# Reading the streamed operand of two chained transformer blocks' matmuls as two interleaved halves

## The chip, the cores and the metric

One core of a Trainium2 chip runs the whole program. The metric is the time of one execution on the device in microseconds, as a median over runs. Engines are named as the profile names them: PE is TensorE's matmul stream, PEld its weight loads, DVE is VectorE, ACT is ScalarE, POOL is GpSimd, SP is the queue that issues DMAs. A matmul has a stationary operand of 128 x 128 (loaded by PEld) and a moving operand of up to 512 columns that streams past it; the sums land in PSUM.

## What is computed

Two transformer blocks on 256 tokens of width 2048, in float32. The first block mixes tokens in three families of heads, then runs a gated convolutional feed-forward (width 5632) and a gated per-layer embedding. The second has a modulation vector, a mixer with windowed and latent attention, and a feed-forward with a squared ReLU (width 8192). Cut to the products around the change:

```
first:   g = conv(h @ w_gate);  y = gelu(g) * (h @ w_up);  x = x + y @ w_down
second:  mod = silu(c) @ w_mod + b_mod          (six rows: sh1, sc1, g1, sh2, sc2, g2)
         u = relu(h @ w_ff1);   x = x + g2 * ((u * u) @ w_ff2)
```

## The kernel before, in words

Weights stream from HBM once. `prep` (lines 273 to 283) fetches one block of 128 x 1024 float32 into `raw`, and splits it into a high part `whi` (ACT, line 281) and a remainder `wlo` (DVE, line 282), both typed float32r. Activations are kept as such pairs too, and each product is three matmuls: high by high, high by low, low by high. There are four `raw` buffers and three of `whi` and `wlo`.

Two helpers issue nearly all matmuls:

- `linear` (lines 297 to 344) has the tokens stationary and the weights moving: 12 matmuls of 512 columns (of 448 or 384 in two chunks) for a block, lines 318, 319, 320. It serves w_in, w_out, w_down, the embedding's products, the second block's w_in2, w_out2, w_ff2, and chunk 0 of ff1. Output has the tokens on partitions.
- `linear_t` (lines 346 to 365) has the weights stationary and the 256 tokens moving: 24 matmuls of 256 columns for a block, lines 360, 361, 362. It serves w_gate, w_up and chunks 1 to 15 of w_ff1. Output has features on partitions and two groups of 256 tokens side by side in a PSUM bank.

Each chunk of 512 outputs is eight blocks. In `linear_t`'s callers the evictions read that bank as `(j t)`: line 984 (gate, DVE), line 1003 (up, DVE), lines 1424 and 1425 (ff1, ACT then DVE).

After each block `tick` (line 250) counts down deferred work that was handed to `spawn`; a deferred piece says after how many ticks it goes on. `tick` also calls `mod_half` at a rate: one of 192 halves of the modulation, a DMA of 512 KB into one of two `wmod` buffers (line 919) and one DVE instruction of 128 x 1024 (line 920). `mod_upto` issues all halves up to a number at once. `mod_row` (lines 935 to 947) adds up a section of the modulation (lines 931, 932), waits 2 ticks, transposes it on PE (line 940), copies it on ACT and spreads it over the partitions through a DRAM row with two kinds of SP DMA.

In `mlp2` the feed-forward runs in four groups of four chunks: ff1 of chunk 4g, then ff2 of the group before, then ff1 of the other three. The last 32 halves of the modulation run at one a tick from the end of ff1's chunk 0. After ff1 of chunk 4 comes `mod_upto(96)`, the `mod_row` for `g2`, and then ff2, whose evictions multiply by `g2`. `out_proj2` calls `mod_row` for `g1` in the same manner.

## Time and profile before

| what | value |
|---|---|
| median of 3 runs | 2290.66 us (2286.03 to 2298.77) |
| profiled execution, its own time | 2293.44 us |
| its span, first to last instruction | 2291.7 us |
| mean granted TensorE clock | 0.993 |
| PE / PEld / DVE / ACT busy | 2246.7 / 1996.9 / 1573.5 / 1105.6 us |
| HBM traffic | 513.38 MB read, 2.14 MB written |

Busy times are sums over instructions. A matmul's row shows its own start and a modelled end, and rows of successive matmuls overlap: the pace of the PE is read from the distance between two starts, not from the duration of one row.

### The profile page before, as it was taken

The page shows a single profiled execution, that of the slowest core. Times are in us where ns is not written, and L with a number is a line of the kernel's source. Part 1 is how long each engine was busy: PE and PEld are TensorE (multiplying, and loading weights), DVE is VectorE, ACT ScalarE, POOL GpSimd, SP SyncE. Part 2 cuts the span into 40 slices and gives each one's busy share as a digit, 9 for nine tenths or more (in the row PEclk, how much of TensorE's full clock was granted, in tenths as well). Part 3 has the DMA queues.
Part 4 walks back from the last instruction along what each step waited for, and adds up shares of the span by engine and source line. Part 5 has one row for each costly group of instructions (what it writes and reads, how often), then busy time and mean ns, then how long its engine had stood idle before and what let it go on. Part 6 is the DMA issues. An engine that isn't in the chain of part 4 may idle for free.

```text
span 2291.7 us, 34932 instructions
## 1 busy us (share of the span) xinstructions
PE 2246.7 (98%) x13714; PEld 1996.9 (87%) x13714; DVE 1573.5 (69%) x2329; ACT 1105.6 (48%) x1560; POOL 25.8 (1%) x35
## 2 busy tenths in 40 slices
PE   9999999999999999999999999999999999999998
PEld 7787887899998999989987788888878998998986
DVE  6777766777876677767777866768766555555555
ACT  6655554454444444434445655655433443443444
POOL 0000000000000000000000000000000000000000
PEclk9999999999999999999999999999999999999999
DMA  8665566677777777777778643566886566656554
GB/s 300 229 211 193 205 230 208 241 254 259 265 264 261 265 252 254 256 258 264 249 255 301 241 161 117 173 194 212 309 290 193 190 187 193 190 187 193 190 188 154
DMA packets 147537, 517.82 MB, mean 226 GB/s; under 512 B 17115, under 2 KB 21292, under 8 KB 146860
## 3 DMA queue, kind: packets, MB, share of 16 engines
q1 hardware_dynamic: 147228, 515.58, 66.3%
q8 instruction: 107, 1.75, 0.3%
q14 instruction: 58, 0.48, 0.1%
q10 hardware_dynamic: 144, 0.01, 0.0%
HBM read 513.38 MB, written 2.14 MB: 225 GB/s over the span
## 4 chain that ended last, share of the span: by engine, by line
PE 80%; DMA 7%; issue 6%; DVE 5%; ACT 1%; POOL 1%; SPq 0%; DVEq 0%; ACTq 0%; POOLq 0%
PE mm L320 14%; PE mm L319 14%; PE mm L318 14%; PE mm L362 11%; PE mm L361 11%; PE mm L360 11%; DMA wmod<-in_w_mod 6%; DVE wlo L282 2%; PE aux L382 1%; DVE wmod L920 1%; PE aux L750 1%; ACT whi L281 1%; DMA raw<-in_w_ff 0%; PE aux L824 0%; PE aux L1273 0%
## 5 line engine op out<-in xcount | busy, mean ns | idle before, releaser
L281 ACT ACTIVATE whi<-raw 128x1024 fp32r<-128x1024 f32 (+1 forms) x746 | 785.9, 1055 | 999.0 <-PE mm L320 539.9
L282 DVE TENSOR_TENSOR wlo<-raw,whi 128x1024 fp32r<-128x1024 f32 (+1 forms) x746 | 905.5, 1216 | 503.6 <-ACT whi L281 501.9
L362 PE MATMUL mm<-xt,wlo 128*128 128x256 f32 x2368 | 662.6, 280 | 5.8 <-DVE wlo L282 5.8
L361 PE MATMUL mm<-xt,whi 128*128 128x256 f32 x2368 | 661.5, 279 | 0.0
L360 PE MATMUL mm<-xt,whi 128*128 128x256 f32 x2368 | 661.5, 279 | 0.0
L361 PEld LDWEIGHTS mm<-xt,whi 128*128 128x128 f32 x2368 | 451.0, 190 | 0.3
L362 PEld LDWEIGHTS mm<-xt,wlo 128*128 128x128 f32 x2368 | 444.6, 188 | 7.4 <-DVE wlo L282 7.2
L360 PEld LDWEIGHTS mm<-xt,whi 128*128 128x128 f32 x2368 | 444.6, 188 | 0.3
L319 PE MATMUL mm<-wlo,hid 128*128 128x512 f32 x848 | 331.4, 391 | 1.0 <-DVE wlo L282 1.0
L318 PE MATMUL mm<-whi,hid 128*128 128x512 f32 x848 | 331.6, 391 | 0.0
L320 PE MATMUL mm<-whi,hid 128*128 128x512 f32 x848 | 331.2, 391 | 0.0
L920 DVE SCALAR_TENSOR_TENSOR wmod<-wmod,cact 128x1024 f32<-128x1024 f32 x192 | 234.5, 1221 | 109.3 <-DMA wmod<-in_w_mod 108.5
L318 PE MATMUL mm<-whi,xt 128*128 128x512 f32 (+2 forms) x660 | 260.3, 395 | 0.9 <-ACT whi L281 0.9
L319 PE MATMUL mm<-wlo,xt 128*128 128x512 f32 (+2 forms) x660 | 256.9, 389 | 3.5 <-DVE wlo L282 3.5
L320 PE MATMUL mm<-whi,xt 128*128 128x512 f32 (+2 forms) x660 | 256.3, 389 | 0.0
L319 PEld LDWEIGHTS mm<-wlo,hid 128*128 128x128 f32 x848 | 159.9, 189 | 35.1 <-DVE wlo L282 2.3
L318 PEld LDWEIGHTS mm<-whi,hid 128*128 128x128 f32 x848 | 159.9, 189 | 33.0
L320 PEld LDWEIGHTS mm<-whi,hid 128*128 128x128 f32 x848 | 159.8, 188 | 33.1
L319 PEld LDWEIGHTS mm<-wlo,xt 128*128 128x128 f32 x660 | 124.5, 189 | 29.3 <-DVE wlo L282 6.6
L318 PEld LDWEIGHTS mm<-whi,xt 128*128 128x128 f32 x660 | 124.3, 188 | 24.6 <-ACT whi L281 1.6
L320 PEld LDWEIGHTS mm<-whi,xt 128*128 128x128 f32 x660 | 124.4, 188 | 23.7
L318 PE MATMUL mm<-whi,mix 128*128 128x512 f32 x244 | 97.9, 403 | 0.0
(349 smaller groups left out, 1796.6 us busy)
## 6 DMA issues: line engine op xcount, KB each, us to landing
raw<-in_w_ff SPq DMA_DIRECT2D x256, 512.0 KB, 3.7
wmod<-in_w_mod SPq DMA_DIRECT2D x192, 512.0 KB, 5.0
raw<-in_w_in SPq DMA_DIRECT2D x120, 512.0 KB, 4.1
raw<-in_w_gate SPq DMA_DIRECT2D x88, 512.0 KB, 3.8
raw<-in_w_up SPq DMA_DIRECT2D x88, 512.0 KB, 4.2
raw<-in_w_down SPq DMA_DIRECT2D x88, 512.0 KB, 4.0
raw<-in_w_out SPq DMA_DIRECT2D x64, 512.0 KB, 3.8
raw<-in_w_pg SPq DMA_DIRECT2D x32, 512.0 KB, 4.6
```

Source lines behind the costliest of these rows:

```text
L281: nc.scalar.activation(hi[:, :ncol], raw[:, :ncol], AF.Copy)
L282: nc.vector.tensor_tensor(lo[:, :ncol], raw[:, :ncol], hi[:, :ncol].bitcast(F32), op=ALU.subtract)
L318: nc.tensor.matmul(o, xh[:, sl], wh, start=st and j == 0, stop=False)
L319: nc.tensor.matmul(o, xh[:, sl], wl, start=False, stop=False)
L320: nc.tensor.matmul(o, xl[:, sl], wh, start=False, stop=en and j == 1)
L360: nc.tensor.matmul(o, hi[:, ws], xh, start=first, stop=False, skip_group_check=True)
L361: nc.tensor.matmul(o, hi[:, ws], xl, start=False, stop=False, skip_group_check=True)
L362: nc.tensor.matmul(o, lo[:, ws], xh, start=False, stop=(b == last and j == 1), skip_group_check=True)
L382: self.nc.tensor.transpose(pt[:, j * P:(j + 1) * P], src[:, j * P:(j + 1) * P], self.ident)
L750: nc.tensor.transpose(pt[:, jo * P:(jo + 1) * P], L[:, j * P:(j + 1) * P], self.ident)
L920: nc.vector.scalar_tensor_tensor(raw, raw, 1.0, self.cact[:, us], op0=ALU.mult, op1=ALU.mult, accum_out=self.macc[:, j, u:u + 1])
```

## The change

The layout of the weights on the host, the order in which moving operands are read, and the place of one deferred piece are changed; no matmul is added or removed. A new function gives a view of a row of columns that reads its two halves in turn (column 0, column n/2, column 1, column n/2 + 1, and so on). In `linear` the host stores each block's columns as all even ones, then all odd ones, so that reading the halves in turn gives the natural order, and outputs stay as they were. In `linear_t` the moving tokens are read in turn, so outputs come out in that order, and the evictions of gate, up and ff1 undo it by reading PSUM at a stride of two elements. `mod_upto(96)` and `mod_row` for `g2` go ahead of ff1's chunk 4 instead of behind it, with a wait of 5 ticks in place of 2. The wait for `g1` stays 2.

```diff
-def _pack(w, widths, nk=2):
+def _pack(w, widths, nk=2, turn=()):
...
-        b = w[:, c0:c0 + cw].reshape(k // (nk * P), nk, P, cw).transpose(0, 2, 1, 3)
+        b = w[:, c0:c0 + cw]
+        if n not in turn:
+            b = np.concatenate([b[:, 0::2], b[:, 1::2]], axis=1)
+        b = b.reshape(k // (nk * P), nk, P, cw).transpose(0, 2, 1, 3)
...
-    a["w_gate"] = _pack(sq("w_gate"), [CW] * NF)
+    a["w_gate"] = _pack(sq("w_gate"), [CW] * NF, turn=range(NF))
...
-    a["w_ff1"] = _pack(sq("w_ff1_2"), [CW] * NF2)
+    a["w_ff1"] = _pack(sq("w_ff1_2"), [CW] * NF2, turn=range(1, NF2))
...
+def moving(w):
+    return w.rearrange("p (a b) -> p b a", a=2)
...
-                wh = w[0][:, j * cw:(j + 1) * cw]
-                wl = w[1][:, j * cw:(j + 1) * cw]
+                wh = moving(w[0][:, j * cw:(j + 1) * cw])
+                wl = moving(w[1][:, j * cw:(j + 1) * cw])
...
-                    xh, xl = xt(2 * b + j)
+                    xh, xl = (moving(x) for x in xt(2 * b + j))
...
-                    evac(m // 2, ps[m // 2].rearrange("p (j t) -> p j t", j=2))
+                    evac(m // 2, ps[m // 2].rearrange("p (j b a) -> p j a b", j=2, a=2))
...
-    def mod_row(self, rows, k0, tmp):
+    def mod_row(self, rows, k0, tmp, wait):
...
-        yield 2
+        yield wait
...
-                    nc.vector.tensor_tensor(g, ps, rb, op=ALU.mult)
+                    nc.vector.tensor_tensor(halves(g), ps, r4, op=ALU.mult)
...
-                    nc.vector.tensor_tensor(y[:, js, :], ps, y[:, js, :], op=ALU.mult)
+                    nc.vector.tensor_tensor(halves(y[:, js, :]), ps, halves(y[:, js, :]), op=ALU.mult)
...
-                    nc.scalar.activation(r, ps, AF.Relu)
-                    nc.vector.tensor_tensor(r, ps, r, op=ALU.mult)
+                    r4 = r.rearrange("p j (a b) -> p j a b", a=2)
+                    nc.scalar.activation(r4, ps, AF.Relu)
+                    nc.vector.tensor_tensor(r4, ps, r4, op=ALU.mult)
...
+                    if g == 1 and n == 0:
+                        self.mod_upto(96)
+                        self.spawn(self.mod_row([g2], 80, F, 5))
                     ff1(4 * g + n)
...
-                    if g == 1 and n == 0:
-                        self.mod_upto(96)
-                        self.spawn(self.mod_row([g2], 80, F))
```

The 30 matmuls of `mixer2`'s latent expansion that have weights moving (lines 1287 and 1312) are changed in the same way, with their weights' layout.

## Rows read from the trace of the kernel before

**Rows 1.** The page: busy time of each engine

```profile
PE 2246.7 (98%) x13714; PEld 1996.9 (87%) x13714; DVE 1573.5 (69%) x2329; ACT 1105.6 (48%) x1560; POOL 25.8 (1%) x35
```

**Rows 2.** Stages by window: time, each engine's busy time (instructions), clock, DMA share, GB/s

```profile
455.00:650.00 195.00, 193.99 (x1651) 191.35 (x1650) 151.50 (x200) 95.20 (x108) 0.70 (x1) 1.00 0.76 261
1576.00:1680.00 104.00, 98.18 (x807) 95.19 (x806) 80.85 (x103) 45.89 (x53) 0.00 (x0) 1.00 0.87 306
```

**Rows 3.** Timeline of PE in the first down projection: start us, us, engine, line, operands

```profile
715.03 0.39 PE L319 MATMUL mm<-wlo,hid 128*128 128x512 f32 x1
...
719.79 0.39 PE L319 MATMUL mm<-wlo,hid 128*128 128x512 f32 x1
```

**Rows 4.** Timeline of PE in gate and up, at two places

```profile
559.74 0.28 PE L360 MATMUL mm<-xt,whi 128*128 128x256 f32 x1
...
564.96 0.28 PE L361 MATMUL mm<-xt,whi 128*128 128x256 f32 x1
...
849.76 0.28 PE L362 MATMUL mm<-xt,wlo 128*128 128x256 f32 x1
...
854.95 0.28 PE L361 MATMUL mm<-xt,whi 128*128 128x256 f32 x1
```

**Rows 5.** Timeline of PE: matmuls whose stationary operand has 12 or 6 columns

```profile
60.14 0.28 PE L565 MATMUL aux<-xt,wb 128*12 128x256 f32 x1
...
60.71 0.28 PE L566 MATMUL aux<-xt,wb 128*6 128x256 f32 x1
```

**Rows 6.** Timeline of PE: attention matmuls whose operands are plain float32

```profile
1385.92 0.60 PE L1247 MATMUL aux<-knT,qnT 128*128 128x256 f32 x2
...
1386.78 0.39 PE L1247 MATMUL aux<-knT,qnT 128*128 128x128 f32 x2
...
1387.23 0.60 PE L1247 MATMUL aux<-knT,qnT 128*128 128x256 f32 x2
```

**Rows 7.** Timeline of PE behind the stall at 1698 us, and that window's row

```profile
1703.11 0.63 PE L319 MATMUL mm<-wlo,hid 128*128 128x512 f32 x1
...
1707.38 0.63 PE L320 MATMUL mm<-whi,hid 128*128 128x512 f32 x1
...
1701.50:1708.00 6.50, 5.50 (x14) 4.34 (x15) 3.24 (x6) 1.32 (x2) 0.00 (x0) 0.50 0.75 284
```

**Rows 8.** Windows of line 318 alone: time, PE (instructions), PEld, clock, DMA, GB/s

```profile
0.00:2291.70 2291.70, 724.87 (x1840) 346.98 (x1840) 0.99 0.67 226
1190.00:1310.00 120.00, 63.53 (x163) 30.45 (x163) 1.00 0.82 286
1310.00:1560.00 250.00, 103.24 (x261) 49.06 (x261) 0.99 0.48 153
```

**Rows 9.** Windows of line 361 alone, columns as above

```profile
455.00:700.00 245.00, 176.84 (x640) 120.15 (x640) 1.00 0.75 259
1550.00:1700.00 150.00, 71.02 (x256) 48.27 (x256) 0.99 0.78 269
700.00:1200.00 500.00, 215.81 (x768) 147.45 (x768) 1.00 0.74 257
1700.00:2300.00 600.00, 197.82 (x704) 135.16 (x704) 0.99 0.58 187
```

**Rows 10.** Evictions and a strided DVE operation, by line: count, duration ns min/median/max

```profile
L984 DVE TENSOR_TENSOR t<-mm,rsb x22: 679/683/692, 492.0 to 1115.1; 128x512 f32<-128x512 f32 x22
L1424 ACT ACTIVATE t<-mm x30: 576/590/603, 1600.9 to 2196.4; 128x512 f32<-128x512 f32 x30
L814 DVE TENSOR_TENSOR E<-E,hkT x28: 280/282/292, 92.8 to 220.6; 128x128 f32<-128x128 f32 x28
```

**Rows 11.** Modulation halves in the second feed-forward (by line, timeline), and a wait of PE

```profile
L919 SPq DMA_DIRECT2D wmod<-in_w_mod x32: 327/328/841, 1575.9 to 1694.3; - x32
1700.80 1.23 DVE L920 SCALAR_TENSOR_TENSOR wmod<-wmod,cact 128x1024 f32<-128x1024 f32 x1 [2.27 <-DMA wmod<-in_w_mod]
PE aux L940 <- DVE modT L932: 3.6, 1, 3.6
```

## The prediction

> **What bounds the kernel now.** I read the page first. PE is busy for 98% of the span and PEld for 87% [rows 1]; but PE's rows overlap and have modelled ends, so this says only that PE seldom stands still, not that its columns run at full pace. The stage table comes next: in the gate and up stage DVE is busy for 151.5 of 195 us and the DMA engines for 0.76 of the time, so neither is the end there, while between 1576 and 1680 us PE has 98.2 of 104 us and the DMA engines 0.87 at 306 GB/s [rows 2]. So PE's pace sets the time almost everywhere, and transfers set it in that one stage. The third view is therefore the distance between starts. In the down projection 21 steps of 512 columns take 4.76 us, 226.7 ns each [rows 3]. At 2.4 GHz 512 columns are 213.3 ns: 13.3 ns, one part in 17, is lost. In gate and up there are two paces: 46 steps in 5.22 us, 113.4 ns, and later 44 steps in 5.19 us, 118.0 ns, against 106.7 [rows 4].

> Three groups of rows say whose loss this is. Matmuls of 256 moving columns with only 12 or 6 stationary columns still take 0.57 us for five steps, 114 ns [rows 5]: it is not the weight load. Plain float32 matmuls take 0.86 us for four of 256 columns, 215 ns each [rows 6], which is 512 columns at 2.4 GHz plus 1.7 ns. I read that as each element being streamed in two passes, so that new elements are asked for half as often, and then nothing is lost. And behind a stall, where the granted clock is 0.50 (1.2 GHz), ten steps of the same 512-column matmul take 4.27 us, 427 ns each [rows 7], which is 512 at 1.2 GHz with nothing lost. So the loss belongs to the moving read of neighbouring float32r elements at full pace, and vanishes where a run of neighbours is walked half as fast. The slower pace of 118.0, with the same instructions, I take for a second clash, between that read and the weight load; which pace holds changes after stalls.

> **The change part by part.** *Moving reads.* In turn, each half is a run of neighbours walked at half the pace, which is what rows 6 and 7 show without loss; unlike there, two runs are walked at once, and no row shows that. Bounds by the nearest rows: 512 columns at 215 ns (rows 6) or with the whole loss gone 213.3, and on the other side 427 (rows 7), should a jump cost the pace of a column. For 256 columns: 107.5, half of the 215, and 112.5, since four plain matmuls of 128 columns in two passes, each with a full weight load, take 0.45 us (rows 6); on the other side 213. I take 215 and 110, because the operand type, the engine and the two-fold walk of rows 6 are nearest.

> Counts: line 318 has 1840 matmuls [rows 8], and lines 319 and 320 as many: 5520, of which all but 192 have 512 columns. Each gains 226.7 - 215 = 11.7 ns, 64.6 us. Of these 163 and 261 a line lie in the embedding and the second mixer [rows 8], 1272 in all and 14.9 us; there PE also waits for transfers (286 GB/s) and for chains through DVE and ACT, so I count half: -7.4. Leaves 57.2 us.

> For `linear_t` line 361 has 640 matmuls before 700 us, 768 and 704 in the later stretches, and 256 between 1550 and 1700 us [rows 9]; times three for its three lines. 1920 go from 113.4 to 110: 6.5 us. The other 4416 lie behind 700 us, where I take the slower pace of rows 4 throughout: from 118.0 to 110, 35.3 us. The 768 in the DMA-bound stage gain nothing: a faster PE only waits there for the same bytes. Leaves 41.8 us.

> *Evictions at a stride of two.* 22 of line 984 and 22 like it of line 1003 at 683 ns, 30 on ACT at 590 ns and 30 on DVE at 683 [rows 10]. Nothing shows a strided PSUM read. The nearest row is DVE's strided read of SBUF: line 814 runs 28 times with runs of 1 to 64 elements and keeps 280 to 292 ns throughout [rows 10]. Bounds: 0, and twice the time, 104 x 0.68 = 71 us of DVE and ACT. I take 0, on the row. Even doubled it hides: 37 passes of `linear_t` last about 22 us each, 71 us are 1.9 us a pass over two engines, and DVE at 151.5 of 195 goes to 0.87 at most; the next pass writes the other two PSUM banks meanwhile. If that cover were gone, the split of the next block (line 282) would be late, and PE at line 362.

> *`mod_row` for g2.* Before, 32 halves are issued between 1575.9 and 1694.3 us, the last DVE instruction on them starts at 1700.8, and PE waits 3.6 us for the transpose behind it [rows 11]; then it runs at 0.50 of the clock for 6.5 us [rows 7], which costs half of that, 3.3. So 6.9 us can go. But the same bytes have to come in the same stage, now with an earlier deadline: 24 halves are out when `mod_upto(96)` issues the other 8 together, on two buffers, ahead of ff1's chunk 4. SP's queue holds the weight blocks behind those that wait for a buffer, the DVE queue holds line 282 behind line 920, and PE then waits at line 362 instead. Worst: 8 x 512 KB at 306 GB/s, 13.7 us, in the open, less the 6.9. I take -3 us: the stage's bytes are unchanged, and about half of the stall with its slow clock should go.

> *Small parts.* The 30 matmuls of the latent expansion gain 0.3 us. `g1`'s wait and the layouts cost nothing on the device; block sizes, and so transfers, are the same.

> **Sum.** 57.2 + 41.8 + 3 = 102.0 us off the profiled execution's 2293.4 gives 2191.4. That execution stands 2.8 us above the median of the runs shown, so against the median the forecast is 2189 us.

> **The rivals.** *Each jump costs a read.* If the unit takes neighbours together and a jump breaks that, columns come at half pace: 427 ns for 512 and 213 for 256. Then 5520 x 200 ns + 1920 x 100 + 4416 x 95 + 768 x 98 = 1104 + 192 + 420 + 75 = 1.79 ms more, some 4080 us. It decides as soon as two successive reads in different places cost more than the one in 17 lost now, that is above 226.7 ns for 512. For it: no row shows a moving operand that jumps. Against it: DVE jumps in SBUF at no cost [rows 10], and the loss seen is of a kind that more time per neighbour removes [rows 6, 7]. [...] I give this case 0.18.

> *The loss stays.* The view is taken, but the read unit fetches just as often, or the limit is a plain rate of 2.26 columns a ns: 226.7 and 113.4 and 118.0 stay. Only `mod_row` is left, 2288 us. For it: 512 over 226.7 could be such a rate. Against it: the matmuls of 256 columns hold two paces. 0.08.

> *Half goes.* [...] Or the full gain comes, and DVE or the transfers take part of it; at 110 ns a block of 24 takes 2.64 us, DVE goes to 0.80 and 261 GB/s to 269, so little. 0.24 for these.

> **How the numbers follow.** The forecast's case (2152 to 2210) has 0.50. Half or a part has 0.24 and lies in 2210 to 2275. Both are faster by over 0.5%, which is 11.5 us and about what a measurement of this kernel can tell: 0.74. The loss stays: within 0.5%, 0.08. Each jump costs: slower, 0.18. The low end takes all of the loss gone without a discount: 5520 x 13.4 = 74, 1920 x 5.9 + 4416 x 10.5 = 57.7, and 6.9 of `mod_row`, 139 off 2293.4, less the 2.8: 2152. The high end takes in the unchanged case with a small loss from `mod_row`: 2300. This leaves out only the jump's 0.18.

> **What would show it.** Right: steps of 512 columns at 213 to 217 ns and of 256 at 107 to 113 with one pace only; lines 984, 1003, 1424 and 1425 at their times; the stage with the last 32 halves as long as now; no wait of 3.6 us at the transpose and no slow clock behind it. Wrong: starts 400 ns apart or more at a granted clock of 1.0 (jumps cost), or 226.7 and 118 again; evictions at 1.2 us, with PE waiting at line 362 for line 282 in gate and up; a new wait of 5 us or more near ff1's chunk 4.

## The result, and the profile after

The changed kernel takes 2220.16 us (2216.61 to 2223.62) beside 2290.44 us before on the same chip: a ratio of 0.9689, 95% interval 0.9657 to 0.9721, or 70 us less. The forecast was 2189, so the direction was right and the gain was seven tenths of what was forecast. The profiled execution took 2216.61 us with a span of 2214.8, 76.8 us under the profiled execution before. Lines from the helpers on stand 10 further down: 318 to 320 are now 328 to 330, 360 to 362 are 370 to 372, 281 and 282 are 291 and 292, 920 is 930; the evictions 984 and 1424 are 996 and 1437.

The page's busy times, to hold against [rows 1]:

```profile
PE 2153.0 (97%) x13714; PEld 1966.8 (89%) x13714; DVE 1567.7 (71%) x2329; ACT 1102.2 (50%) x1560; POOL 25.8 (1%) x35
```

PE lost 93.7 us of busy time and the span only 76.9: some of what PE gained became waiting. The timeline of PE (start us, duration us, engine, line, operands) in the first down projection, which answers to [rows 3]:

```profile
699.76 0.38 PE L330 MATMUL mm<-whi,hid 128*128 128x512 f32 x1
...
704.50 0.38 PE L328 MATMUL mm<-whi,hid 128*128 128x512 f32 x1
```

These are 22 steps in 4.74 us, 215.5 ns; over the whole trace such a step takes 215.8 ns, where it took 226.7. The same view in gate and up, at the two places of [rows 4]:

```profile
559.81 0.28 PE L372 MATMUL mm<-xt,wlo 128*128 128x256 f32 x1
...
564.95 0.28 PE L370 MATMUL mm<-xt,whi 128*128 128x256 f32 x1
...
849.28 0.28 PE L370 MATMUL mm<-xt,whi 128*128 128x256 f32 x1
...
854.42 0.28 PE L371 MATMUL mm<-xt,whi 128*128 128x256 f32 x1
```

Both times 46 steps in 5.14 us, 111.7 ns. The second, slower pace of [rows 4] is gone: there is one pace for 256 columns, from the first block of gate to the last of ff1.

The evictions by line (count, duration ns min/median/max, first and last start), which answer to [rows 10]:

```profile
L996 DVE TENSOR_TENSOR t<-mm,rsb x22: 679/683/690, 477.0 to 1078.0; 128x512 f32<-128x512 f32 x22
L1437 ACT ACTIVATE t<-mm x30: 570/578/598, 1553.5 to 2123.8; 128x512 f32<-128x512 f32 x30
```

Reading PSUM at a stride of two costs neither DVE nor ACT anything: 683 ns as before, and 578 beside 590.

The waits of PE (engine, line, what it waited for: us in total, times, longest), the first three in the kernel before:

```profile
PE mm L362 <- DVE wlo L282: 5.8, 7, 2.0
PE mm L319 <- DVE wlo L282: 5.4, 7, 1.1
PE aux L382 <- DVE hn L1101: 5.1, 2, 2.7
```

And in the changed kernel, the last of which answers to [rows 11]:

```profile
PE aux L392 <- DVE hn L1113: 9.2, 3, 5.0
PE mm L329 <- DVE wlo L292: 8.8, 16, 1.5
PE mm L372 <- DVE wlo L292: 8.5, 11, 1.5
...
PE aux L950 <- DVE modT L942: 3.6, 1, 3.6
```

And the timeline of PE at that transpose, the one of `mod_row`, which answers to [rows 7]:

```profile
1655.42 0.28 PE L950 MATMUL aux<-ident,modT 128*16 128x128 f32 x1 [3.62 <-DVE modT L942]
...
1656.30 0.63 PE L328 MATMUL mm<-whi,hid 128*128 128x512 f32 x1
...
1658.86 0.63 PE L328 MATMUL mm<-whi,hid 128*128 128x512 f32 x1
```

The stall of 3.6 us stands where it stood, and the steps behind it are still at the lower clock: six in 2.56 us, 427 ns each (426.7, or 1.2 columns a ns), at a granted clock of 0.50. The transpose is the 10156th matmul in both traces, and the weight blocks and halves are issued in the same order: the edit moved `mod_row` in the source, and the order of the queues came out the same. The waits for the remainder of a weight block grew: 8.5 us in 11 at line 372, where line 362 had 5.8 in 7, and 8.8 in 16 at line 329, where line 319 had 5.4 in 7. At line 392 PE waits for the normalized activations of the second block: 9.2 us in 3 where it was 5.1 in 2, the longest, 5.0 us for 2.4, at the end of the embedding.

The traces were then cut at the same counts of matmuls on both sides, so that each stage can be set against itself:

| stage | before, us | after, us | gain |
|---|---|---|---|
| w_in and w_out | 461.1 | 445.4 | 15.7 |
| gate/up, chunks 0 to 4 | 220.4 | 219.5 | 0.9 |
| gate/up, chunks 5 to 10 | 271.4 | 257.8 | 13.6 |
| the three passes of down | 242.4 | 231.3 | 11.1 |
| embedding | 107.1 | 109.4 | -2.2 |
| w_in2 and w_out2 with the mixer | 245.8 | 237.6 | 8.2 |
| ff1, chunk 0 | 24.2 | 23.4 | 0.8 |
| ff1, chunks 1 to 4 | 97.4 | 99.4 | -2.0 |
| ff1, chunks 5 to 15 | 248.6 | 235.7 | 12.9 |
| the four passes of ff2 | 356.7 | 339.0 | 17.7 |

Two stages became longer, the embedding and ff1's chunks 1 to 4, both full of transfers (a DMA share of 0.84 and 0.86 in the windows further down). The table is of one execution on each side, and these two stages vary: in the profiled executions of this kernel and of those below that leave the stage as it is here, the embedding took 108.7 to 115.0 us and ff1's chunks 1 to 4 took 97.6 to 100.8, so the signs hold better than the sizes. So three questions were open: why the gain per step is what it is (the prediction's reason was untested), what the move of `mod_row` does, and what the two stages give back to.

### The profile page after: what moved, and what is told of

Same layout as the page of the kernel before. It is cut to its first block, busy times and chain, and to the rows that moved or that the text cites. A ratio compares the mean times of both kernels' runs of the same rounds, so it can differ in the third digit from the quotient of the medians.

```text
span 2214.8 us, 34936 instructions
## 1 busy us (share of the span) xinstructions
PE 2153.0 (97%) x13714; PEld 1966.8 (89%) x13714; DVE 1567.7 (71%) x2329; ACT 1102.2 (50%) x1560; POOL 25.8 (1%) x35
## 4 chain that ended last, share of the span: by engine, by line
PE 62%; DMA 7%; issue 6%; DVE 3%; ACT 1%; SPq 0%; POOL 0%; ACTq 0%; POOLq 0%; DVEq 0%
PE mm L372 10%; PE mm L371 10%; PE mm L370 10%; PE mm L330 9%; PE mm L328 9%; PE mm L329 9%; DMA wmod<-in_w_mod 6%; DVE wlo L292 2%; PE aux L392 0%; DMA raw<-in_w_ff 0%; PE aux L760 0%; PE aux L1285 0%; DVE wmod L930 0%; ACT whi L291 0%; PE aux L1236 0%
## 5 line engine op out<-in xcount | busy, mean ns | idle before, releaser
L372 PE MATMUL mm<-xt,wlo 128*128 128x256 f32 x2368 | 653.1, 276 | 8.7 <-DVE wlo L292 8.5
L371 PE MATMUL mm<-xt,whi 128*128 128x256 f32 x2368 | 651.4, 275 | 0.0
L370 PE MATMUL mm<-xt,whi 128*128 128x256 f32 x2368 | 651.3, 275 | 0.0
L372 PEld LDWEIGHTS mm<-xt,wlo 128*128 128x128 f32 x2368 | 454.5, 192 | 11.5 <-DVE wlo L292 11.3
L371 PEld LDWEIGHTS mm<-xt,whi 128*128 128x128 f32 x2368 | 454.6, 192 | 0.2
L370 PEld LDWEIGHTS mm<-xt,whi 128*128 128x128 f32 x2368 | 454.6, 192 | 0.2
L329 PE MATMUL mm<-wlo,hid 128*128 128x512 f32 x848 | 322.4, 380 | 1.2 <-DVE wlo L292 1.2
L328 PE MATMUL mm<-whi,hid 128*128 128x512 f32 x848 | 322.5, 380 | 0.0
L330 PE MATMUL mm<-whi,hid 128*128 128x512 f32 x848 | 322.3, 380 | 0.0
L329 PE MATMUL mm<-wlo,xt 128*128 128x512 f32 (+2 forms) x660 | 250.0, 379 | 5.9 <-DVE wlo L292 5.6
L328 PE MATMUL mm<-whi,xt 128*128 128x512 f32 (+2 forms) x660 | 252.5, 383 | 1.2 <-ACT whi L291 1.2
L330 PE MATMUL mm<-whi,xt 128*128 128x512 f32 (+2 forms) x660 | 248.3, 376 | 0.0
L329 PE MATMUL mm<-wlo,mix 128*128 128x512 f32 x244 | 93.0, 381 | 1.9 <-DVE wlo L292 1.9
```

Of the source, the lines that this page charges most:

```text
L328: nc.tensor.matmul(o, xh[:, sl], wh, start=st and j == 0, stop=False)
L329: nc.tensor.matmul(o, xh[:, sl], wl, start=False, stop=False)
L330: nc.tensor.matmul(o, xl[:, sl], wh, start=False, stop=en and j == 1)
L370: nc.tensor.matmul(o, hi[:, ws], xh, start=first, stop=False, skip_group_check=True)
L371: nc.tensor.matmul(o, hi[:, ws], xl, start=False, stop=False, skip_group_check=True)
L372: nc.tensor.matmul(o, lo[:, ws], xh, start=False, stop=(b == last and j == 1), skip_group_check=True)
```

## The experiments

**One part at a time.** Three kernels, each the changed kernel with one part undone: `mod_row` back behind chunk 4; the tokens in natural order (weights alone in turn); the weights in natural order (tokens alone in turn). The edits of the last two are cut to one line each; the layouts and evictions go with them.

```diff
 e1: -                    if g == 1 and n == 0:
     -                        self.mod_upto(96)
     -                        self.spawn(self.mod_row([g2], 80, F, 5))
                          ff1(4 * g + n)
     ...
     +                    if g == 1 and n == 0:
     +                        self.mod_upto(96)
     +                        self.spawn(self.mod_row([g2], 80, F, 2))
     ...
 e2: -                    xh, xl = (moving(x) for x in xt(2 * b + j))
     +                    xh, xl = xt(2 * b + j)
     ...
 e3: -                wh = moving(w[0][:, j * cw:(j + 1) * cw])
     +                wh = w[0][:, j * cw:(j + 1) * cw]
     ...
```

> The changed kernel with mod_row for g2 and mod_upto(96) back behind ff1's chunk 4, waiting 2 ticks; reads stay in turn. Theory (the move does nothing, because the transpose stands at the same place of PE's queue and the last modulation half lands no sooner): 2220 us, within 4 us, with the 3.6 us wait before the transpose and the slow clock behind it as in the changed kernel. Rival (the move saves part of the stall, as the prediction's -3 says): 2223 to 2227 us, with a longer wait at the transpose.

Measured: 2222.42 us, ratio 0.9689 (0.9664 to 0.9714), the changed kernel's own ratio; the transpose is the 10156th matmul here too, and PE waits 3.0 us for it. No effect of the move can be seen.

> The changed kernel with the tokens of gate, up and ff1 read in their natural order and evicted without a stride; weights still in turn. Theory (each read order sets the pace of its own matmuls alone): 512 columns at 215.8 ns, 256 columns back at 113.3 or 117.8, and the stages of linear_t as long as before: 2220 + 25 = 2245 us. Rival (the pace of 256 columns came from something else that changed, such as the evictions or the timing of transfers): 256 columns stay at 111.7 and the time at 2220.

Measured: 2239.87 us, 0.9771 (0.9739 to 0.9804). The timeline of PE in gate and up of this kernel:

```profile
559.83 0.28 PE L372 MATMUL mm<-xt,wlo 128*128 128x256 f32 x1
...
564.93 0.28 PE L372 MATMUL mm<-xt,wlo 128*128 128x256 f32 x1
...
849.28 0.28 PE L370 MATMUL mm<-xt,whi 128*128 128x256 f32 x1
...
854.46 0.28 PE L372 MATMUL mm<-xt,wlo 128*128 128x256 f32 x1
```

45 steps in 5.10 us and 44 in 5.18: the paces of 113.3 and 117.7 ns are back. So turning the tokens is what removes the second pace.

> The changed kernel with the weights of linear read in their natural order (and stored so); tokens of gate, up and ff1 still in turn. Theory: 512 columns at 226.7 ns, 256 at 111.7, 2220 + 51 = 2271 us. Rival (a shared cause): both paces move together. If the two parts' gains don't add up, the sum of this and the run with weights alone differs from 70 us by more than 6.

Measured: 2257.28 us, 0.9841 (0.9814 to 0.9867): 256 columns at 111.7 ns and 512 at 226.7. The timeline of PE in gate and up, and in the first down projection:

```profile
559.81 0.28 PE L371 MATMUL mm<-xt,whi 128*128 128x256 f32 x1
...
564.95 0.28 PE L372 MATMUL mm<-xt,wlo 128*128 128x256 f32 x1
...
714.72 0.39 PE L330 MATMUL mm<-whi,hid 128*128 128x512 f32 x1
...
719.94 0.39 PE L329 MATMUL mm<-wlo,hid 128*128 128x512 f32 x1
```

46 steps in 5.14 us and 23 in 5.22. It was 14 us faster than expected, and the kernel with the weights alone 5 us. The parts gain 53.0 and 35.6 us on the kernel before that was measured beside them, 88.6 together, and the whole 70. Some 6 us of the surplus can be read: with the weights alone, ff1's chunks 5 to 8 and 13 to 15 happen to run at the faster of the two paces, where the kernel before had 117.8 ns throughout. The timeline of that kernel in chunk 5 and in chunk 9:

```profile
1744.75 0.28 PE L370 MATMUL mm<-xt,whi 128*128 128x256 f32 x1
...
1749.96 0.28 PE L371 MATMUL mm<-xt,whi 128*128 128x256 f32 x1
...
1914.83 0.28 PE L370 MATMUL mm<-xt,whi 128*128 128x256 f32 x1
...
1919.89 0.28 PE L371 MATMUL mm<-xt,whi 128*128 128x256 f32 x1
```

46 steps in 5.21 us, 113.3 ns, and 43 in 5.06, 117.7, and PE waits for nothing between 1745 and 2220 us. The rest of the surplus stays open.

**Why in turn is free.** Next the order of reading was varied, since the prediction's reason (a run walked at half pace loses nothing) makes a forecast for other orders: four runs in turn, eight runs, a stride of two, pairs of neighbours from the two halves. The chunks of the down projection (512 columns) and of gate and up (256) each got another order, with the host's layout and the evictions to match.

```diff
-def moving(w):
-    return w.rearrange("p (a b) -> p b a", a=2)
+def moving(w, o="h2"):
+    if o == "c":
+        return w
+    if o == "s2":
+        return w.rearrange("p (b a) -> p a b", a=2)
+    if o == "p2":
+        return w.rearrange("p (a b e) -> p b a e", a=2, e=2)
+    return w.rearrange("p (a b) -> p b a", a=int(o[1:]))
...
+DOWN = ("p2", "h4", "s2", "h8")
+UP = ("h2", "h4", "s2", "h8", "c")
```

> The changed kernel with other orders in places: the four chunks of w_down read halves in turn by pairs of neighbours, quarters in turn, every second column and then the others (stride two, one run at a time), and eighths in turn; gate and up's chunks 0 to 4 read halves, quarters, stride two, eighths, and natural order. Theory A (the loss goes wherever a run of neighbours is walked at half pace or slower): pairs, quarters and eighths at 216 ns for 512 columns, quarters and eighths at 111.7 for 256; natural order at 113.3 or 117.8. Theory B (the loss comes once for each stretch of 16 neighbours passed, however it is walked): stride two passes twice as many stretches, 240 ns for 512 and 120 for 256; under theory C (two direct neighbours in succession are what costs) stride two loses nothing, 216 and 111.7, and pairs stay between 216 and 227.

Measured: 2499.07 us. The timeline of PE in the four chunks of the down projection, two rows of each (pairs, quarters, stride of two, eighths):

```profile
774.78 0.51 PE L354 MATMUL mm<-whi,hid 128*128 128x512 f32 x1
...
782.78 0.51 PE L354 MATMUL mm<-whi,hid 128*128 128x512 f32 x1
...
806.81 0.45 PE L352 MATMUL mm<-whi,hid 128*128 128x512 f32 x1
...
814.74 0.45 PE L353 MATMUL mm<-wlo,hid 128*128 128x512 f32 x1
...
835.46 0.63 PE L353 MATMUL mm<-wlo,hid 128*128 128x512 f32 x1
...
844.93 0.63 PE L353 MATMUL mm<-wlo,hid 128*128 128x512 f32 x1
...
879.60 0.67 PE L354 MATMUL mm<-whi,hid 128*128 128x512 f32 x1
...
889.82 0.67 PE L354 MATMUL mm<-whi,hid 128*128 128x512 f32 x1
```

24 steps in 8.00 us, 28 in 7.93, 21 in 9.47 and 21 in 10.22: 333, 283, 451 and 487 ns at a granted clock of 1.0. With 256 columns, halves took 111.7 ns, quarters 143, a stride of two 229, eighths 220 and the natural order 117.8. Of these orders only two runs in turn keep 111.7 ns (215.8 for 512 columns). The prediction's reason falls, since runs walked at a quarter or an eighth of the pace should lose less still, and every theory of this expectation falls with it.

Two more explanations were tried before a better one was found. One: what counts is how far apart the two runs lie, or that the view has one more level. The halves were cut into 2 to 32 groups, each read as two halves in turn:

```diff
-    return w.rearrange("p (a b) -> p b a", a=2)
+    return w.rearrange("p (g a b) -> p g b a", g=g, a=2)
...
+DOWN = (2, 4, 8, 16)
+UP = (2, 4, 8, 16, 32)
```

> The changed kernel with the two runs that alternate put closer together: the moving columns are read in groups, each as two halves in turn. The four chunks of w_down have 2, 4, 8 and 16 groups, so the two runs lie 128, 64, 32 and 16 elements apart (256 in the changed kernel); up's chunks 0 to 4 have 2, 4, 8, 16 and 32 groups, 64, 32, 16, 8 and 4 elements apart (128 there). Theory D (two reads in succession go side by side when they fall in places far enough apart; the pairs of neighbours lost because two neighbours do not): 216 and 111.7 hold down to some distance and below it the pace falls to 300 ns and more for 512 columns. Theory E (two alternating runs are free at any distance): 216 and 111.7 throughout. Theory F (a third level in the read pattern is what cost the pairs of neighbours): all grouped reads lose, 330 ns and 160.

Measured: 2219.22 us, with 215.8 and 111.7 ns in every group: runs 128 down to 16 elements apart with 512 columns, and 64 down to 4 with 256, cost the same. The other: that the last 5 ns of a 256-column step are a clash of addresses between tokens and weights, which an offset of the weight tile would move (`sh` is the offset in elements, one value per chunk of gate and up, in place of 16 throughout):

```diff
...
+                sh = (16, 0, 4, 8, 12, 20, 24, 32, 40, 48, 64)[c]
-                self.linear_t(xg, "w_gate", c * D * CW, conv)
+                self.linear_t(xg, "w_gate", c * D * CW, conv, sh)
```

> The changed kernel with the stationary weights of gate and up at another offset in their tile for each of chunks 0 to 10: 16 (as now), 0, 4, 8, 12, 20, 24, 32, 40, 48 and 64 elements. Theory (111.7 ns for 256 columns is what a weight load of 128 columns takes, whatever its address): 111.7 at each offset. Rival (the offset that suited the read in natural order now costs, and another one lets 256 columns run at 107 to 109): at least one offset below 110. Third: with the read in natural order two paces were seen; if the clash with the weight load is still there at some offsets, those show 115 or more.

Measured: 2226.49 us, and 111.7 ns at every offset. No clash that an offset of the weights moves is left; that the weight load sets this pace would fit, but wasn't shown.

**Two streams.** The paces measured for 512 columns fit one more reading, which is the author's and which no trace shows at work: count odd and even columns as two streams, and let each lose when it leaves an aligned group of four elements (16 bytes) before it has read all four in succession. In turn, each stream reads four neighbours (215.8 ns). In natural order each reads every second element, two of a group (226.7). At a stride of two it is one of a group (451); with quarters, eighths and pairs every read of a stream changes the group (283 to 487). This makes a sharp forecast: runs 2 apart, or runs 4 apart that begin 8 bytes into a group, should lose the whole gain again, though they are two runs in turn like the others. The last kernel of this line gave the four down chunks these four cases (groups, and offset of the tile in elements), and up's chunks 0 to 3 runs 2 and 4 apart by turns:

```diff
+DOWN = ((128, 0), (64, 0), (64, 2), (128, 2))
+UP = (64, 32, 64, 32)
...
-                w = self.prep(src[0], 2 * cw)
+                w = self.prep(src[0], 2 * cw, shift=DOWN[c][1] if name == "w_down" else 0)
```

> The changed kernel with the two alternating runs closer still, or off their alignment. The four chunks of w_down: runs 2 elements apart; 4 apart; 4 apart with the weights' tile begun 2 elements (8 bytes) later; 2 apart, also begun 2 elements later. Up's chunks 0 to 3: 2, 4, 2 and 4 elements apart. Lane theory (the odd and the even columns of a matmul are read by two separate streams; each stream loses when it takes fewer than four elements in succession from the same 16 bytes: two in the natural order, one at stride two): 4 apart 216, 2 apart as slow as natural order, 226.7 (113.3 or 117.8 in up), and 4 apart begun 2 elements later 226.7 too, since each stream then takes two elements from each 16 bytes. Rival (two alternating runs are free whatever the distance): 216 and 111.7 throughout.

Measured: 2228.42 us. The timeline of PE in the four chunks (2 apart; 4 apart; 4 apart begun 8 bytes later; 2 apart begun 8 bytes later):

```profile
679.67 0.39 PE L337 MATMUL mm<-whi,hid 128*128 128x512 f32 x1
...
684.89 0.39 PE L339 MATMUL mm<-whi,hid 128*128 128x512 f32 x1
...
699.82 0.38 PE L337 MATMUL mm<-whi,hid 128*128 128x512 f32 x1
...
705.00 0.38 PE L337 MATMUL mm<-whi,hid 128*128 128x512 f32 x1
...
719.66 0.39 PE L338 MATMUL mm<-wlo,hid 128*128 128x512 f32 x1
...
724.88 0.39 PE L337 MATMUL mm<-whi,hid 128*128 128x512 f32 x1
...
739.84 0.39 PE L337 MATMUL mm<-whi,hid 128*128 128x512 f32 x1
...
744.82 0.39 PE L338 MATMUL mm<-wlo,hid 128*128 128x512 f32 x1
```

23 steps in 5.22 us, 24 in 5.18, 23 in 5.22, 22 in 4.98: 227, 216, 227 and 226 ns. The same order loses its whole gain when it begins 8 bytes later. In up, runs 2 apart took 113.3 ns and runs 4 apart 111.7. All four cases, and both in up, came as forecast, and the rival on record, that two alternating runs are free at any distance, is out. The runs don't tell two streams from columns that are taken two at a time: the same counts follow from both.

**What is given back.** In the embedding and in ff1's chunks 1 to 4 the halves of the modulation come in beside the weights. If they take the gain, fewer of them there should free it. The first kernel lets the 32 halves of the second feed-forward come at 0.62 a tick and puts `mod_row` and the first ff2 one chunk later; the second also has more of them out ahead of the embedding (0.42 a tick in the first block in place of 0.36: 166 of 192, not 143); the third goes on to 0.46 (182) and 0.5. The third's edit:

```diff
-                    self.mod_rate = 0.36
+                    self.mod_rate = 0.46
...
-                        self.mod_rate = 1.0
-                    if n == 0 and pend is not None:
+                        self.mod_rate = 0.5
+                    at = 1 if g == 1 else 0
+                    if g == 1 and n == 1:
+                        self.mod_upto(96)
+                        self.spawn(self.mod_row([g2], 80, F, 6))
+                    if n == at and pend is not None:
```

> The changed kernel with the last 32 halves of the modulation at 0.62 a tick in place of 1.0, and ff2 of the first group, mod_upto(96) and mod_row for g2 behind ff1's chunk 5 in place of chunk 4. Theory (the part of the gain that was given back in this stage went to transfers at 300 GB/s, and to the wait at the transpose): the 13 us that PE stands still in ff1's chunks 1 to 4 go to 4 or less, and the 7.6 us in ff2 of the first group to 1 or less: 2220 - 15 = 2205 us. Rival (those stalls are not of the transfers): no change, 2220.

Measured: 2213.83 us, 0.9672 (0.9650 to 0.9694): less was gained than expected, and the interval overlaps the changed kernel's. In the profiled execution the time that PE stands still in ff1's chunks 1 to 4 fell from 13.7 us to 8.4, not to 4, and in ff2 of the first group from 7.6 to 4.0, not to 1.

> As the run with ff2 later, and the rate of the modulation's halves in the first block at 0.42 a tick in place of 0.36, so that fewer are left to be fetched together ahead of the embedding. Theory (the embedding's stage lost 2 us to before because its weights queue behind those halves): its 12 us of stalls fall by 6 or more, 2199 us. Rival (the embedding is held by other things, or gate and up now lose what it gains): within 2 us of the run without the rate.

Measured: 2208.87 us, 0.9639 (0.9596 to 0.9682). This is 5.0 us under the kernel with the old rate, where 6 were expected of the rate, with intervals that overlap. In the profiled executions the embedding took 103.3 us, where it took 109.6 with the old rate.

> The changed kernel itself once more, beside the run below: 2220 us within 4 us.

Measured: the changed kernel again, beside the next one: 2224.64 us (2222.94 to 2229.69), 0.9707 (0.9682 to 0.9732), 0.6 us above the stretch expected.

> The run with ff2 later, with 0.46 halves a tick in the first block and 0.5 in the second feed-forward: 182 of the 192 halves are then out before the embedding, and 10 are left for the second feed-forward, where 18 of 160 were left for the embedding and 32 for the feed-forward in the changed kernel. Theory (what was given back went to transfers in these two places): 2204 us or less, ff1's chunks 1 to 5 with 3 us of stalls in all, and gate and up with no more than 3 us of new ones. Rival (gate and up, at some 285 GB/s, lose as much): 2212 or more.

Measured: 2208.52 us (2201.80 to 2214.77), 0.9636 (0.9611 to 0.9661). The intervals of these two don't overlap: this version beats both kernels, the changed one by 16 us. The time lies between the theory's 2204 and the rival's 2212, and is no better than that of the second kernel, 2208.87: that the last step of the rates gains anything isn't shown. The windows of the changed kernel (us; busy of PE, PEld, DVE, ACT, POOL with instructions; clock; DMA share; GB/s) in most of the embedding and in ff1's chunks 1 to 3:

```profile
1173.00:1270.00 97.00, 89.52 (x403) 75.95 (x402) 74.91 (x96) 51.02 (x65) 1.02 (x2) 0.97 0.84 287
1530.00:1605.00 75.00, 68.72 (x590) 66.74 (x589) 57.83 (x75) 32.09 (x38) 0.00 (x0) 1.00 0.86 299
```

The same windows of the last kernel, columns as above:

```profile
1173.00:1270.00 97.00, 93.09 (x431) 81.63 (x430) 63.28 (x71) 57.82 (x76) 2.54 (x3) 0.97 0.69 222
1530.00:1605.00 75.00, 72.88 (x636) 72.04 (x635) 55.15 (x66) 37.87 (x44) 0.00 (x0) 1.00 0.80 275
```

And in that kernel line 930 alone, the DVE work on the halves (its busy time with instructions, two a half, since one of 0.08 us stands behind each of 128 x 1024; clock; DMA share; GB/s):

```profile
1173.00:1270.00 97.00, 0.00 (x0) 0.97 0.69 222
1530.00:1605.00 75.00, 12.29 (x20) 1.00 0.80 275
```

No half and ten halves are left in these windows, where the changed kernel had 15 and 19. PE is busy 3.6 and 4.2 us more in the same time. By stages, ff1's chunks 1 to 3 go from 74.1 us to 67.8, near the 64.3 that their 576 matmuls need at 111.7 ns, and the embedding from 109.4 to 103.2, which the second kernel had reached. The wait for `hn` at the embedding's end only shrinks from 5.0 us to 3.9, so most of what is won there comes from the blocks before it, and 1.5 us of what the change added at that place the halves don't explain: from the embedding's last eviction through DVE to `hn` it takes 5.7 us in the kernel before, 5.7 in the changed one and 5.9 in this one, and PE comes to the end of its other work 4.2 us behind that eviction before, 1.6 in the changed kernel and 2.9 in this one. Some 4 us come back as waits at the end of the first block (the last pass of down and gate/up 9 and 10), where the halves now are.

## Why the prediction was right, and where it was wrong

**The direction and the main mechanism held.** The loss belongs to the order of the moving reads, reading in turn removes it but for 2.5 ns of 512 columns and 5 of 256 (215.8 for 213.3, 111.7 for 106.7), and the second pace of 256 columns goes with it. No trace gives a clock in GHz: the prediction's 2.4 GHz, and its 213.3 and 106.7, can be worked out from the steps at a granted clock of 0.50, which take 427 ns in natural order [rows 7] and 426.7 in turn. Half of that is 213.3, if a column takes half as long at a clock of 1.00 and nothing is lost at 0.50; that the two orders agree there shows only that the order costs nothing at half the clock.

**The reason given was wrong.** The step that failed is that the loss "vanishes where a run of neighbours is walked half as fast". Quarters walk each run at a quarter of the pace and take 283 ns. What goes with the pace in the orders tried is how many reads in succession odd and even columns, counted as two streams, each take from one aligned group of 16 bytes: four at 215.8 ns, two at 226.7, one at 283 to 487. Of the rows from which the reason came, rows 7 show 427 ns at half the clock, and rows 6 show 215 ns for 256 plain float32 columns; that these are streamed in two passes was the author's reading, and no run shows it. Neither could tell two runs in turn from one run slowed down.

**The rival "each jump costs a read"** did not happen in the change's order: successive columns lie 128 or 256 elements apart there, and the steps take 111.7 and 215.8 ns. Had the change read at a stride of two or in eighths, it would have come true: 451 and 487 ns for 512 columns and 229 and 220 for 256 are above the rival's own 427 and 213; pairs (333) and quarters (283 and 143) lie short of it. No row read before the change told an order that costs from one that doesn't, so 0.18 for this case was not too much.

**Steps of 512 columns:** 215 forecast, 215.8 measured, which is 4.4 us over 5520. The stages with weights moving gained 51.2 us, where the sum had 57.2. The half discount was near in total, 6.0 us for 7.4, but not where: the second mixer's two products gained 8.2 us, more than the 4.6 allowed, and the embedding lost 2.2 where some 3 were counted as gain.

**Steps of 256 columns:** 110 forecast, 111.7 measured. Over 6336 steps this is 10.6 us, the largest term that was off. The working named 112.5 from rows 6 as the other end and took the value nearer to no loss; the measured pace lies next to that end. Gate and up and ff1 gained 25.4 us, where the sum had 41.8. That the pace "changes after stalls" is not the whole of it: in the kernel before it goes from 113.3 ns in gate and up's chunk 4 to 117.8 in chunk 5 with only a down pass between, and PE waits for nothing from 560 to 855 us. That the second pace is a clash with the weight load, as the prediction took it, no run shows.

**The stages bound by transfers** were counted as unchanged. They became longer: ff1's chunks 1 to 3 by 3.4 us and the embedding by 2.2, and in gate/up 0 to 3 waits took 2.2 of the 2.6 that the pace gave. A faster PE ahead of such a stage lets `tick` issue the halves of the modulation sooner, and they and the weights then share the queue in less time. That halves and weights compete there is shown by runs that differ in the rates alone (the embedding from 109.6 to 103.3, ff1's chunks 1 to 3 from 72.0 to 67.8; all but the 1.5 us at the embedding's end); that the ticks' earlier issue is what made it worse than before is argued from the order of the work.

**`mod_row`:** -3 forecast, 0 measured. The step assumed that moving the call in the source moves the work; the queues came out in the old order, and the 3.6 us of [rows 11] stayed.

**Evictions at a stride of two:** 0 forecast, 0 measured.

From the sum: 102.0 less 10.6 and 0.9 (256 columns: 111.7 for 110, and 117.8 where 118.0 was taken), less 4.4 (512), less 3.0 (`mod_row`), less 9.3 (embedding 5.1, gate/up 0 to 4 2.2, ff1's chunks 1 to 4 2.0), plus 3.6 (mixer) is 77, beside the 76.8 between the two profiled executions. The terms of the transfer stages are those of one execution; in the repeat of the changed kernel the embedding alone took 5.7 us more.

**The range.** The paces are those of the case that had 0.50, but the time is not: 2220 lies 10 us above its 2210, in the stretch that was given to "half or a part" at 0.24. That case names the full gain with transfers taking part of it, though as little; that half of the loss stays did not happen: of the 13.4 ns lost in 226.7, 10.9 went. All the terms that moved but the mixer's came out lower than forecast, 25 us in all, and it is the width of the range that held their sum.

## What to carry to other kernels

When every step of a matmul runs a few per cent over its columns (here 226.7 ns for 213.3), look at the order in which the moving operand is read: of those tried with these float32r operands, the fastest (215.8 ns) took odd and even columns each as four neighbours from one aligned group of 16 bytes, and cost only a layout on the host or a view in the eviction. Before you trust such a mechanism, vary the order: neighbouring orders that look as good cost up to 2.3 times the time (487 ns for 215.8), and 8 bytes of offset can take the gain back (227 ns for 216). After a gain in pace, look for the stages bound by transfers and move deferred transfers away from them; this gave another 16 us here.
